# Closing rows with VectorE's copy and a third row begun ahead, and rotation with the sine at the eviction, in a two-layer encoder on one core

## Chip, core and metric

The kernel runs on one core of one Trainium2 chip. The metric is the device time of one execution in microseconds (us): the median of several runs. Engines: PE is TensorE (matmuls and transposes), DVE is VectorE, ACT is ScalarE, POOL is GpSimd, and SP issues the DMA transfers. PE writes its results to PSUM, a small memory of eight banks; DVE and ACT read it from there. The other memory that the engines share is SBUF.

## The reference, cut to what matters

512 tokens of 1024 features pass through two layers, each with three residual additions, and a last norm:

```
for l in range(DEPTH):
    x = x + hybrid_mixer(rms_norm(x, norm_mix[l]), w_in[l], ..., w_out[l])
    x = x + memory_cross_attention(rms_norm(x, norm_mem_q[l]), rms_norm(mem, ...), ...)
    x = x + conv_ffn(rms_norm(x, norm_ffn[l]), w_up[l], conv_w[l], conv_b[l], w_down[l])
return rms_norm(x, norm_final)
```

The mixer has two head groups on one projection. Eight heads do neighbourhood attention over the 8 by 64 token grid (a softmax over 256 neighbours of each block, with a learned bias). Eight query heads and two key heads of 64 features do grouped attention: each head of q and k is normalised over its 64 features and then rotated,

```
out = stack([x1 * c - x2 * sn, x1 * sn + x2 * c])
```

where x1 and x2 are groups of 16 features of the normalised head and c, sn are cosine and sine of a position. Both groups' outputs are put side by side and multiplied by w_out. Everything is float32.

## The kernel before, in words

**Layout.** x lies transposed in SBUF (`xT[c]`, eight tiles of 128 features by 512 tokens). A float32 matrix product is made of three products of rounded parts: each operand is split into hi (rounded) and lo (the rest), and hi times hi, hi times lo and lo times hi are accumulated in one PSUM bank. Weights are read by DMA as `raw`; hi comes from ACT (L265) and lo from POOL (L266), some steps ahead of use. `get_w` takes the next weight of the plan and issues the following transfers and splits.

**Order of the work.** A scheduler decides the order of each engine's instructions from the program's order and priorities; `behind(n)` shifts the priority of what is in it (negative: earlier). Attention is written as a weave: units of work pass through stages (scores, normalise, transpose, values), and between their stages a filler issues pieces of projection matmuls, so that PE has work while the other engines are at softmax. `late(n, f)` calls f n ticks of the filler later. A tick is a few matmuls long.

**PSUM.** Four banks hold matmul results (`mm`), two scores (`sc`), two transposes and small results (`tr`). Accesses of two engines to one bank follow each other in program order, reads too. A bank is free for the next product when its last reader is done.

**Closing rows.** A row is one of eight 128-feature slices of a product that is added to x; 12 matmuls of 512 columns make one. `Norm.close` (L425) is called for 40 rows: the eight of the mixer's output and the eight of memory attention in both layers, and the eight of layer 0's last product. It adds x in PSUM (L428, DVE), makes the next stage's operand hi on ACT (L438) and lo on DVE (L440), copies the sum to `xT` (L430, ACT) and squares it for the norm's statistic (L444, ACT). `close_rows` (L960) runs the last quarter of the mixer's product: rows 0 and 1 are begun when the first two parts of the attention output are there and continued with the third; the fourth part, which goes through `fold` (L481: ACT copy L486, DVE add L488; later ACT L491 and POOL L492), is waited for. When it is there, all eight rows are closed one after the other.

**Neighbourhood values.** `na_values` (L775) multiplies the split values with the split probabilities into a bank whose four parts (two halves of partitions by two terms) must be added: ACT copies one half of partitions out (L789, 64 by 512), DVE adds the other half to it (L790), and DVE adds the two terms (L791).

**Rotation.** Each of four pairs of query heads and the pair of key heads is projected into one bank by `gqa_project`, and then `gqa_rope` (L835) makes three things from it: xs = gain times the bank (ACT, L840), sq = its square (ACT, L841), cc = gain times the bank times the cosine (DVE, L842). One tick later `swap` starts four DMAs that exchange groups of 32 partitions of xs, PE adds the squares of a head with eight small matmuls (operand `pairs`), and DVE makes the variance v (L852, L855). One tick later `rotate` has POOL take the power -1/2 (L862), spread it over rows (L863), multiply the swapped xs by the sine (L864) and add cc (L865). Two ticks later `norm` transposes the rows by a matmul with the identity, and one tick later DVE multiplies and the result is split. `gqa_tables` (L803) scales cosine and sine tables by the mixer norm's factor at the start of a layer (POOL, L805) and makes its square r2 (L807).

## Time and profile before

| what | value |
|---|---|
| runs | 1388.48, 1388.41, 1386.73 us |
| median | 1388.41 us |
| profiled execution | 1388.67 us |
| its span, first to last instruction | 1386.4 us |
| mean granted clock of TensorE | 0.992 |
| ACT copy to xT in a closing row (L430), x38 | 0.590 us |
| ACT square in a closing row (L444), x38 | 0.611 us |
| ACT xs, sq (L840, L841), x10 each | 0.690, 0.590 us |
| DVE cc (L842), x10 | 0.751 us |
| POOL sine product, sum (L864, L865), x10 each | 1.296, 1.287 us |

The profile is of one execution; its times are those of the median run within 0.3 us. A line of the waits names an engine, its operation and line, then what it waited for (engine, tile, line) with total, number and longest in us. A stretch's line has its bounds, its length and then each engine's busy time with the number of instructions, TensorE's granted clock (1.00 is full speed), the DMA engines' share and GB/s. A timeline's line has start, duration, engine, line, operation, output and inputs, shape, and in brackets the engine's idle time before it and what ended it. Names such as `mm`, `tr`, `sc`, `t` (a temporary), `s` (a small tile), `xg` (the operand's halves) and `r` (a rounded tile) are tiles. "ident" is the identity matrix, used to transpose.

### The profile page before, as it was taken

The numbers are of one execution on the slowest core, as the hardware profiler recorded it, in microseconds if no ns is written. First come the engines' busy times: TensorE is split into PE (matmuls) and PEld (weight loads), VectorE is DVE, ScalarE is ACT, GpSimd is POOL, SyncE is SP. The second block draws the span as 40 slices with busy tenths as digits, with TensorE's granted clock in tenths as the row PEclk, the third lists the DMA queues.
The fourth block names the chain that finished last, engine by engine and source line by source line (L and its number), as shares of the span: only waits on it lengthen the run. The fifth ranks groups of instructions, "written<-read, shape, count | busy, mean of one in ns | idle before, by whom it ended". The sixth has DMA issues, their size and how long they took to land.

```text
span 1386.4 us, 19225 instructions
## 1 busy us (share of the span) xinstructions
PE 1355.3 (98%) x7072; PEld 1157.1 (83%) x7072; DVE 838.3 (60%) x1462; ACT 703.8 (51%) x1305; POOL 719.7 (52%) x537
## 2 busy tenths in 40 slices
PE   8999999999999999999999989999999999999997
PEld 7898789787888888888888978898788888888897
DVE  6666666363787187358446557754638833861874
ACT  6766577655443144234557657766654422432441
POOL 2458876635444444444645678756264444444441
PEclk9999999999999999999999999999999999999998
DMA  7753312322333333333356523223133333333331
GB/s 213 202 145 86 86 57 78 92 62 61 106 97 102 91 94 95 101 100 89 109 147 166 139 74 99 62 75 109 54 90 100 91 104 94 90 93 107 95 89 61
DMA packets 218205, 138.83 MB, mean 100 GB/s; under 512 B 6016, under 2 KB 211072, under 8 KB 218112
## 3 DMA queue, kind: packets, MB, share of 16 engines
q1 hardware_dynamic: 217968, 137.60, 34.9%
q8 instruction: 56, 0.92, 0.3%
q14 instruction: 37, 0.30, 0.1%
q10 hardware_dynamic: 144, 0.00, 0.0%
HBM read 125.00 MB, written 2.10 MB: 92 GB/s over the span
## 4 chain that ended last, share of the span: by engine, by line
PE 88%; ACT 4%; DVE 3%; POOL 2%; DMA 2%; issue 1%; SPq 0%; DVEq 0%; ACTq 0%; POOLq 0%
PE mm L77 79%; PE sc L77 5%; PE tr L64 3%; PE tr L77 1%; ACT hi L265 1%; DMA raw<-in_w_in 1%; POOL lo L266 1%; DMA raw<-in_w_down 1%; DVE s L900 1%; POOL r L266 0%; DMA xT<-in_xT 0%; ACT t L902 0%; DVE t L455 0%; DVE xg L473 0%; ACT t L745 0%
## 5 line engine op out<-in xcount | busy, mean ns | idle before, releaser
L266 POOL TENSOR_TENSOR lo<-raw,hi 128x1024 fp32r<-128x1024 f32 (+2 forms) x268 | 499.7, 1876 | 496.0 <-ACT hi L265 476.0
L77 PE MATMUL mm<-xg,hi 128*128 128x512 f32 x1920 | 595.5, 391 | 1.4 <-DVE t L842 1.4
L77 PEld LDWEIGHTS mm<-xg,hi 128*128 128x128 f32 x1920 | 357.4, 188 | 73.3 <-DVE t L842 1.6
L265 ACT CAST hi<-raw 128x512 fp32r<-128x512 f32 (+2 forms) x276 | 224.5, 837 | 349.0 <-PE mm L77 277.5
L77 PE MATMUL mm<-xg,lo 128*128 128x512 f32 x960 | 374.3, 390 | 0.0
L77 PE MATMUL mm<-r,hi 128*128 128x512 f32 (+1 forms) x1144 | 333.9, 376 | 4.4 <-ACT t L444 2.2
L77 PEld LDWEIGHTS mm<-r,hi 128*128 128x128 f32 x1144 | 209.2, 190 | 42.7 <-ACT t L444 3.1
L1202 DVE SCALAR_TENSOR_TENSOR t<-t,par,t 128x7 f32<-128x7 f32 (+1 forms) x352 | 201.9, 641 | 34.0 <-ACT t L1195 34.0
L77 PE MATMUL mm<-r,lo 128*128 128x512 f32 (+1 forms) x572 | 214.3, 375 | 0.0
L77 PEld LDWEIGHTS mm<-xg,lo 128*128 128x128 f32 x960 | 180.7, 188 | 38.1
L77 PEld LDWEIGHTS mm<-r,lo 128*128 128x128 f32 x572 | 108.5, 190 | 19.1
L1187 DVE TENSOR_TENSOR t<-mm,rep 128x512 f32<-128x512 f32 x88 | 60.1, 687 | 78.2 <-PE mm L77 62.3
L479 POOL TENSOR_SCALAR t<-t,s 128x512 f32<-128x512 f32 (+1 forms) x112 | 66.1, 607 | 75.1 <-DVE s L908 37.2
L1204 ACT ACTIVATE t<-t 128x512 f32<-128x512 f32 x44 | 27.9, 633 | 134.5 <-DVE t L1202 134.5
L1208 DVE TENSOR_TENSOR r<-t,r 128x512 fp32r<-128x512 f32 x44 | 90.5, 2056 | 7.3 <-ACT r L1207 4.1
L1231 DVE TENSOR_TENSOR xT<-xT,mm 128x512 f32<-128x512 f32 x32 | 21.9, 685 | 106.8 <-PE mm L77 106.8
L77 PE MATMUL sc<-r,r 128*128 128x256 f32 (+1 forms) x352 | 71.3, 334 | 0.4 <-ACT t L902 0.3
L64 PE MATMUL tr<-ident,t 128*128 128x128 f32 x456 | 63.3, 275 | 8.5 <-DVE r L473 2.8
L1195 ACT ACTIVATE t<-t,par 128x512 f32<-128x512 f32 x88 | 66.8, 806 | 3.2 <-DVE t L1187 3.2
L64 PEld LDWEIGHTS tr<-ident,t 128*128 128x128 f32 x456 | 52.0, 141 | 18.7 <-issue 6.9
L77 PE MATMUL mm<-r,r 128*128 128x256 f32 (+1 forms) x428 | 62.1, 297 | 0.1
L77 PEld LDWEIGHTS mm<-r,r 128*128 128x128 f32 x428 | 56.1, 191 | 2.7 <-POOL r L266 0.3
(155 smaller groups left out, 1598.8 us busy)
## 6 DMA issues: line engine op xcount, KB each, us to landing
raw<-in_w_up SPq DMA_DIRECT2D x88, 512.0 KB, 3.9
raw<-in_w_in SPq DMA_DIRECT2D x33, 512.0 KB, 4.5
raw<-in_w_down SPq DMA_DIRECT2D x32, 448.0 KB, 3.8
raw<-in_w_mem_kv SPq DMA_DIRECT2D x16, 512.0 KB, 3.9
raw<-in_w_down SPq DMA_DIRECT2D x16, 512.0 KB, 4.2
r<-in_bias SPq DMA_DIRECT2D x16, 384.0 KB, 6.2
r<-r SPq DMA_DIRECT2D x22, 256.0 KB, 5.3
raw<-in_w_out SPq DMA_DIRECT2D x8, 512.0 KB, 3.6
```

What stands on the lines that cost most here:

```text
L64: return lambda *a, **k: self.tc.keep_in_program_order(op(*a, **k))
L77: return self.tc.keep_in_program_order(self.engine.matmul(out, lhsT, rhs, **k))
L265: act.copy(hi[:, k], raw[:, k])
L266: (POOL if eng[0] == "P" else DVE).tensor_sub(lo[:, k], raw[:, k], f(hi)[:, k])
L479: eng.tensor_scalar(e, e, sums[:, col : col + 1], 1.0, op0=ALU.mult, op1=ALU.mult)
L900: DVE.tensor_reduce(nmx[:, c], sc[j], axis=AX.X, op=ALU.max, negate=True)
L1187: DVE.tensor_mul(u, us[side], ffn.rep)
L1195: ACT.activation(cc, u, AF.Identity, bias=par[:, l, CB + ch : CB + ch + 1], scale=w[1])
L1202: DVE.scalar_tensor_tensor(cc[:, dst], u[:, src], wi, cc[:, dst], op0=ALU.mult, op1=ALU.add)
L1204: ACT.activation(cs[0], cs[0], AF.Silu)
L1208: DVE.tensor_sub(acts[j][1], cs[0], f(acts[j][0]))
L1231: DVE.tensor_add(xT[m], xT[m], pm)
```

## The change

Four edits:

1. `close` copies the sum to `xT` with DVE, right after the add and ahead of hi and lo; the square reads `xT`.
2. `close_rows` begins a third row (its first three parts) before it closes the first.
3. `na_values` copies only one term's half out with ACT, and DVE adds the other two pieces straight out of PSUM; the tile `tt` goes.
4. In `gqa_rope` the sine is multiplied at the eviction, on DVE, so that the swapped xs needs only the addition; the tables are no longer scaled by the norm's factor. Instead epsilon is scaled (`gqa_eps`): the variance that the norm's own `rsqrt` had made is kept (`mix.var`) and multiplied by the epsilon of q and k. v is then one DVE operation instead of two, and the small matmuls, v, the power and the rows are all in `rotate`, one tick later than before. The sign of the sine table is turned to fit.

The diff, cut to its core:

```diff
@@ Norm
             DVE.tensor_add(pm, pm, xT[c])
+            DVE.tensor_copy(xT[c], pm)
             self.operand(c, src=pm)
-            ACT.copy(xT[c], pm)
-            self.square(c, src=pm)
+            self.square(c)
@@ na_values
-                ACT.copy(th[r], po[64:128])
-                DVE.tensor_add(tt[r], po[0:64], th[r])
-            DVE.tensor_add(o32s[p][...], tt[:, :, 0], tt[:, :, 1])
+                ACT.copy(th[r, :, 0], po[64:128, :, 0])
+                DVE.tensor_add(th[r, :, 1], po[0:64, :, 1], th[r, :, 0])
+                DVE.tensor_add(o32[r], po[0:64, :, 0], th[r, :, 1])
@@ gqa_tables, gqa_eps
-            for i in range(2):
-                POOL.tensor_mul(gtab[0][:, i], gtab[0][:, i], mix.rep)
-            r2.append(small(NB))
-            POOL.tensor_mul(r2[0], mix.rstd, mix.rstd)
+            for i, e in enumerate((EPS, EPS * HD)):
+                DVE.tensor_scalar(geps[:, i], mix.var, e, None, op0=ALU.mult)
@@ gqa_rope
-                ACT.activation(xs, pm, AF.Copy, scale=gain)
+                DVE.scalar_tensor_tensor(xs, pm, gain, gtab[0][:, 1], op0=ALU.mult, op1=ALU.mult)
+                DVE.scalar_tensor_tensor(cc, pm, gain, gtab[0][:, 0], op0=ALU.mult, op1=ALU.mult)
                 ACT.activation(sq, pm, AF.Square)
-                DVE.scalar_tensor_tensor(cc, pm, gain, gtab[0][:, 0], op0=ALU.mult, op1=ALU.mult)
             def swap():
                 xr = tmp()
                 for i in range(4):
                     SP.dma_start(xr[32 * i : 32 * i + 32], xs[32 * (i ^ 1) : 32 * (i ^ 1) + 32])
+                late(1, lambda: rotate(xr))
+            def rotate(xr):
                 pv = ps_t()
                 for b in range(NB):
                     PE.matmul(pv[:, 2 * b : 2 * b + 2], sq[:, b * P : (b + 1) * P], pairs, start=True, stop=True)
-                v = small(2 * NB)
-                DVE.tensor_tensor(v..., pv..., r2[0].unsqueeze(2).to_broadcast([P, NB, 2]), op=ALU.mult)
-                DVE.tensor_scalar(v, v, ..., op0=ALU.mult, op1=ALU.add)
-                late(1, lambda: rotate(xr, v))
-            def rotate(xr, v):
-                r = small(2 * NB)
+                v, r = small(2 * NB), small(2 * NB)
+                DVE.scalar_tensor_tensor(v..., pv..., 1.0 / HD if g == "k" else 1.0, geps[...], op0=ALU.mult, op1=ALU.add)
                 rows = tmp()
                 with behind(-40):
                     POOL.tensor_tensor(r, v, mhalf[:, : 2 * NB], op=ALU.pow)
                     POOL.tensor_copy(rows..., r.unsqueeze(2).to_broadcast([P, 2 * NB, HD]))
-                POOL.tensor_mul(xr, xr, gtab[0][:, 1])
                 POOL.tensor_add(xr, cc, xr)
@@ close_rows
+            def begin(m):
+                if m // 2 == len(w):
+                    w.append(get_w(("outg", 0, m // 2)))
+                rows.append((ps_mm(), w[m // 2], slice(P * (m % 2), P * (m % 2) + P)))
+                gemm_T(*rows[m][:2], ops, range(3), 0, 3, rows[m][2])
+            begin(n)
             for m in range(KC):
-                if m < n:
-                    pm, ws, c = rows[m]
-                    gemm_T(pm, ws, ops, [3], 0, 3, c)
-                else:
-                    ...
-                    gemm_T(pm, w[m // 2], ops, range(4), 0, 3, slice(P * (m % 2), P * (m % 2) + P))
+                if m == len(rows):
+                    begin(m)
+                pm, ws, c = rows[m]
+                gemm_T(pm, ws, ops, [3], 0, 3, c)
                 norm.close(m, pm)
```

The number of matmuls is the same in both kernels.

More of the change, by code (lines that the diff above doesn't have):

```diff
@@ L379, in encoder_kernel @@
     gfin = cpool.tile([P, KC], F32, name="gfin")
+    geps = cpool.tile([P, 2, NB], F32, name="geps")
     def load_parameters():
@@ L403, in rsqrt @@
             POOL.tensor_tensor(r, v, mhalf[:, :n], op=ALU.pow)
-        return r
+        return r, v
     def row_rep(rstd, n, tag, bufs):
@@ L440, in operand, with square @@
                 dve.scalar_tensor_tensor(lo, src, g, f(hi), op0=ALU.mult, op1=ALU.subtract)
-        def square(self, c, act=ACT, eng=None, src=None):
+        def square(self, c, act=ACT, eng=None):
             sq = tmp((self.n,))
-            act.activation(sq, xT[c][:, self.cols] if src is None else src, AF.Square)
+            act.activation(sq, xT[c][:, self.cols], AF.Square)
             eng = eng or (POOL if self.gcol is not None and c < KC - 1 else DVE)
@@ L464, in stat @@
                     PE.matmul(pv[:, b : b + 1], self.last[:, bs], ones, start=False, stop=True)
-            self.rstd = rsqrt(pv[:, 0:nb], nb, 1.0 / D, factor)
+            self.rstd, self.var = rsqrt(pv[:, 0:nb], nb, 1.0 / D, factor)
         def spread(self):
@@ L779, in na_values @@
                 o32s[p] = tmp()
-            th, tt = tmp((2, 2, P)), tmp((2, 2, P))
+            th = tmp((2, 2, P))
+            o32 = o32s[p][:, 256 * bp : 256 * bp + 256].rearrange("p (i q) -> p i q", i=2)
             for j in range(2):
@@ L788, in na_values @@
                 r = slice(64 * j, 64 * j + 64)
-                ACT.copy(th[r], po[64:128])
-                DVE.tensor_add(tt[r], po[0:64], th[r])
-            DVE.tensor_add(o32s[p][:, 256 * bp : 256 * bp + 256].rearrange("p (i q) -> p i q", i=2), tt[:, :, 0], tt[:, :, 1])
+                ACT.copy(th[r, :, 0], po[64:128, :, 0])
+                DVE.tensor_add(th[r, :, 1], po[0:64, :, 1], th[r, :, 0])
+                DVE.tensor_add(o32[r], po[0:64, :, 0], th[r, :, 1])
             if bp == 1:
@@ L797, in na_values, with gqa_eps @@
                     vblk[p // 2] = None
-        gq, gk, gvt, gtab, r2 = [None] * 4, [], [], [], []
-        def gqa_tables():
-            for i in range(2):
-                POOL.tensor_mul(gtab[0][:, i], gtab[0][:, i], mix.rep)
-            r2.append(small(NB))
-            POOL.tensor_mul(r2[0], mix.rstd, mix.rstd)
+        gq, gk, gvt, gtab = [None] * 4, [], [], []
+        def gqa_eps():
+            for i, e in enumerate((EPS, EPS * HD)):
+                DVE.tensor_scalar(geps[:, i], mix.var, e, None, op0=ALU.mult)
         def gqa_project(g):
@@ L850, in swap @@
                     PE.matmul(pv[:, 2 * b : 2 * b + 2], sq[:, b * P : (b + 1) * P], pairs, start=True, stop=True)
-                v = small(2 * NB)
-                DVE.tensor_tensor(v.rearrange("p (b j) -> p b j", j=2), pv[:, 0 : 2 * NB].rearrange("p (b j) -> p b j", j=2),
-                                  r2[0].unsqueeze(2).to_broadcast([P, NB, 2]), op=ALU.mult)
-                DVE.tensor_scalar(v, v, *((1.0 / HD, EPS) if g == "k" else (1.0, EPS * HD)), op0=ALU.mult, op1=ALU.add)
-                late(1, lambda: rotate(xr, v))
-            def rotate(xr, v):
-                r = small(2 * NB)
+                v, r = small(2 * NB), small(2 * NB)
+                DVE.scalar_tensor_tensor(
+                    v.rearrange("p (b j) -> p b j", j=2), pv[:, 0 : 2 * NB].rearrange("p (b j) -> p b j", j=2),
+                    1.0 / HD if g == "k" else 1.0, geps[:, int(g != "k")].unsqueeze(2).to_broadcast([P, NB, 2]),
+                    op0=ALU.mult, op1=ALU.add)
                 rows = tmp()
@@ L978, in close_rows @@
             norm = norm()
-            for m in range(KC):
-                if m < n:
-                    pm, ws, c = rows[m]
-                    gemm_T(pm, ws, ops, [3], 0, 3, c)
-                else:
-                    if m // 2 == len(w):
-                        w.append(get_w(("outg", 0, m // 2)))
-                    pm = ps_mm()
-                    gemm_T(pm, w[m // 2], ops, range(4), 0, 3, slice(P * (m % 2), P * (m % 2) + P))
+            def begin(m):
[4 more added lines that the diff above has]
+            begin(n)
+            for m in range(KC):
+                if m == len(rows):
+                    begin(m)
+                pm, ws, c = rows[m]
+                gemm_T(pm, ws, ops, [3], 0, 3, c)
                 norm.close(m, pm)
@@ L1034, in na_quanta @@
                 SP.dma_start(gtab[0], t["rope"])
-                gqa_tables()
+                gqa_eps()
             return [NA_FILL] * 3
@@ L1312, in _rope_tables @@
     c, s = np.cos(ang).reshape(S, 2 * nf).T, np.sin(ang).reshape(S, 2 * nf).T
-    tab = np.stack([np.concatenate([c, c, c, c]), np.concatenate([-s, s, -s, s])], axis=1)
+    tab = np.stack([np.concatenate([c, c, c, c]), np.concatenate([s, -s, s, -s])], axis=1)
     return np.ascontiguousarray(tab.astype(np.float32))
```

## The prediction

> **What bounds the kernel now.** I read the page first (busy shares, the chain that ended last), then the waits of PE, then the stretches around each wait, then the timelines of PE, ACT, POOL and DVE there. The profiled execution took 1388.67 us, 0.26 over the median of 1388.41; its span is 1386.4, so 2.3 us lie around it. All sums below are made against 1388.67.

> ```profile
> PE 1355.3 (98%) x7072; PEld 1157.1 (83%) x7072; DVE 838.3 (60%) x1462; ACT 703.8 (51%) x1305; POOL 719.7 (52%) x537
> ...
> PE 88%; ACT 4%; DVE 3%; POOL 2%; DMA 2%; issue 1%; SPq 0%; DVEq 0%; ACTq 0%; POOLq 0%
> ```

> PE is the bound. The change issues the same matmuls, so only PE's stalls can move, and the other engines count only where one of them is late for PE. The waits of PE (engine, line, waited for: total, times, longest):

> ```profile
> PE tr L64 <- DVE r L473: 2.8, 2, 1.9
> PE tr L77 <- ACT t L841: 2.6, 2, 1.3
> PE mm L77 <- ACT t L444: 2.2, 2, 1.1
> PE tr L64 <- DVE xg L473: 2.0, 2, 1.6
> PE mm L77 <- POOL r L492: 1.9, 1, 1.9
> ...
> PE mm L77 <- DVE t L842: 1.4, 1, 1.4
> ...
> PE tr L64 <- POOL t L479: 1.3, 2, 0.8
> PE mm L77 <- POOL t L863: 1.2, 1, 1.2
> ```

> Nearly all of them lie in four places that the diff touches: the rotary part (L841, L842, L863, and transposes queued near it), the closing rows (L492, L444). A stall has a second price, seen in PE's stretches cut at 3.41 us (busy times of PE, PEld, DVE, ACT, POOL; then the granted clock):

> ```profile
> 145.52:148.93 3.41, 2.18 (x9) 2.18 (x10) 2.26 (x6) 1.97 (x5) 3.41 (x4) 0.50 0.73 190
> 247.92:251.33 3.41, 1.32 (x7) 0.80 (x6) 0.48 (x1) 2.13 (x5) 3.41 (x4) 1.00 0.00 0
> 251.33:254.75 3.42, 3.42 (x9) 2.69 (x9) 2.05 (x3) 0.99 (x2) 2.14 (x2) 0.50 0.54 161
> 817.95:821.36 3.41, 1.50 (x10) 1.20 (x9) 2.53 (x5) 2.18 (x6) 1.44 (x2) 1.00 0.32 72
> 821.36:824.77 3.41, 3.41 (x10) 2.61 (x9) 2.05 (x3) 1.00 (x2) 2.55 (x2) 0.50 0.02 5
> 841.84:845.25 3.41, 1.77 (x11) 1.30 (x10) 3.33 (x6) 3.38 (x9) 3.41 (x7) 1.00 0.09 22
> 845.25:848.66 3.41, 3.41 (x18) 2.87 (x19) 2.90 (x6) 2.57 (x7) 3.41 (x4) 1.00 0.00 0
> ```

> The stretches that follow 1.32 and 1.50 us of busy PE ran at clock 0.50; the one that follows 1.77 ran at 1.00. In the half-clock stretches PE lost a further 1.9 us (251.3), 1.4 (821.4) and 1.95 (148.5 to 152.3), by the excess of its start-to-start times over the usual 0.227 us of a 512-column matmul. So a stall near 1.9 us costs about 3.5 in all, one of 1.6 only itself. [...]

> **The closing rows, one row.** Before: DVE add 0.70 (L428), ACT hi 0.69 (L438), DVE lo 0.75 (L440), ACT copy 0.59 (L430), ACT square 0.61 (L444), which frees the bank: 3.34 us. After: the copy is on DVE and stands ahead of hi. No row shows a DVE copy out of PSUM; its bounds are 0.42 (L488, an add on half the columns) and 0.75 (L440), and I take 0.69, by the row it is nearest to, L428's add of the same shape. Square now reads SBUF and holds no bank. [...] The bank is freed at 0.70 + 0.69 + 0.69 + 0.75 = 2.83 us, 0.5 earlier, while lo, which the next stage reads, is 0.7 later. DVE's load per row goes from 1.45 to 2.14 us, under PE's 2.72 (12 matmuls), so DVE does not become the bound; without that margin each of 40 rows would add the excess.

> At 322.4 and 1000.65 PE waited 1.28 us each for L444 to free a bank. The first bank now comes 0.3 earlier: **-0.6** for both (nothing to -1.0).

> **The third row, layer 0.** The timeline there:

> ```profile
> 247.80 2.52 POOL L266 TENSOR_TENSOR lo<-raw,hi 128x512 fp32r<-128x512 f32 x2 [5.36 <-ACT hi L265]
> ...
> 250.28 0.71 POOL L492 TENSOR_TENSOR r<-t,r 128x256 fp32r<-128x256 f32 x1
> ...
> 251.05 0.58 PE L77 MATMUL mm<-r,hi 128*128 128x512 f32 x1 [1.95 <-POOL r L492]
> ```

> The last part of the third k waits on POOL's fold, which stands behind two weight folds. The loss was 0.30 + 2.22 + 1.9 at half clock = 4.4. After, nine matmuls of the third row (9 x 0.227 = 2.04 us) run from about 248.46 to 250.50, and 0.5 is left, with no half clock: -3.9. But the order of ACT's instructions changes: the split of the first memory-query weight (L265) now stands ahead of the first row's hi, since hi waits for one more DVE step.

> ```profile
> 252.83 0.69 ACT L438 ACTIVATE xg<-mm,par 128x512 fp32r<-128x512 f32 x1 [2.75 <-DVE mm L428]
> 254.45 1.05 ACT L265 CAST hi<-raw 128x1024 fp32r<-128x1024 f32 x1 [0.94 <-DMA raw<-in_w_mem_q]
> ```

> That split waits for a DMA that landed at 254.45 (issued at 250.34, when POOL freed the raw tile, which the change does not move). So hi of row 0 runs from 255.5 to 256.2, lo to 256.95, and the fifth row, which needs the first row's bank at about 255.55, waits 1.4. Net **-2.5** (-3.9 if the split does not hold hi back, -0.8 if this stall takes the clock too).

> **The same in layer 1.** There is no stall to win. In that layer too the split (937.00 to 938.05, waiting for its DMA) now stands ahead of hi; hi ends at 938.75, lo at 939.5, and the fifth row wants the bank at 937.76: **+1.75** (0 to +3.45, with 1.7 for a half-clock stretch; 1.75 lies between the 1.64 that did not set it off and the 1.91 that did).

> **The neighbourhood values.** ACT's copy goes from 0.58 (L789) to 0.37 (L486, the same shape), 32 times; DVE's 0.68 + 0.43/2 becomes 2 x 0.42 (L488). ACT gains 6.7 us beside PE, DVE breaks even, PE waits for neither at this line: 0. If their cover were gone this would be worth 0.2 a unit.

> **The rotary part.** POOL loses ten multiplications of 1.30 (L864) and four of 1.30 (L805), 18 us beside PE. DVE takes xs at 0.75 (nearest row L842; L840 on ACT took 0.69), ACT keeps sq, now behind both DVE reads. Bank and pairs operand come within 0.1 of before (0.75 + 0.75 + 0.59 against 0.69 + 0.59 + 0.75). The pairs' eight small matmuls, the one DVE step on them (0.17 to 0.22 by L852, L855, where two stood), POOL's power (1.65) and rows (0.62) are issued one tick later, so PE's wait for sq (142, 830) goes, but POOL's power now queues behind two more weight folds of 1.25 (L266). SP's swap transfers stay where they were.

> Layer 0: the stalls at 100.9 (0.40), 110.5 (0.13) and 133 (1.03), and 0.9 at the pairs, go by the order: some 2.4 up to the last projection, which ends at T0 = 141.1. From there, before: the last norm (ident matmuls) at T0 + 11.6. After, counted from an end 2.4 earlier: POOL's L266 pair to +3.2, power to +4.85, rows to +5.5; PE is there at +2.75, so it stalls about 2.7, probably with a half-clock stretch; the last norm comes at +12.3 to 13, which is T0 + 9.9 to 10.6. Gain 1.0 to 1.7. The wait for L479 at 162 (1.18) is filled by six more matmuls: gain 1.0. Together **-2.4** (-4 to +0).

> Layer 1, an estimate with the same rows: the waits at 817.9 (2.07, and 1.4 of clock) and 830.1 (1.49) go: -4.96. New: the third q head's norm waits 2.2 for POOL's rows (which come 5.5 after the end of the last projection, PE at 3.2), half the time with a stretch of 1.7 (+0.85), and transposes behind DVE's later step, the two small score products that stood ahead of them covering 0.96 of it: +0.96. The 1.8 at 843 stays. Net **-1.0** (-5 to +4).

> Sum: -2.5 + 1.75 - 0.6 - 2.4 - 1.0 = -4.75, so 1388.67 - 4.75 = 1383.9. FFN (340 to 690, 1020 to 1340) loses nothing before and nothing after.

> **Rivals.**
> 1. *The weight split in front of hi costs a clock stretch in both layers.* -2.5 + 1.7, +1.75 + 1.7, the rest as above: -1.35, 1387.3: no change to measure. For it: 1.75 is near the edge. Against: 1.4 is not.
> 2. *The late tick of the pairs: POOL's rows hold PE at the norms of the last two q heads.* Decides from where rows come over 1.9 after PE. In layer 1, where neither norm waited before, 2.2 and 2.4 with 1.65 of clock each are +7.9 against -4.96: +2.9; layer 0 comes out at 0, and the fifth row in layer 1 takes its stretch: -2.5 + 3.45 - 0.6 + 0 + 2.9 = +3.25, so 1391.9, slower. For it: POOL is busy for all 3.41 us of the stretch at 841.84. Against: POOL has 1.30 less to do for each head.
> 3. *The split does not hold hi back* (its DMA lands earlier, or hi is off the path): -3.9 + 0 - 0.6 - 2.4 - 1 = -7.9, and with layer 1 at -3, -9.9: about 1379.
> 4. *The change does not do what it says:* the third row could be begun too late to cover the fold. The order of PE's instructions puts its nine matmuls ahead of the last parts, and the bank that they need came free at 247.36, so I give this nothing; it would be the forecast without -3.9 + 1.4 = 2.5, or 1386.4.

> **How the numbers follow.** Forecast 0.48, rival 1 0.20, rival 2 0.22, rival 3 0.10. Time 1383.9. The range 1379 to 1393 takes in rivals 1 and 2 and the edge of 3; the open bounds of the rotary part alone are some 9 us wide. About 0.2% (2.8 us) is what a measurement of this kernel can tell from no change. Faster: forecast, rival 3, less the forecast's upper edge: 0.55; within: 0.21; slower: 0.24.

> **What would show it.** In the changed kernel: no wait for L492's fold over 0.6 and clock 1.00 after 251; ACT's weight split ahead of the first L438 at both closings and a fifth row waiting 1.4 and 1.75 for lo; waits for L444's square gone from PE's list and replaced by lo's line at 0.9 to 1.0; no PE wait for sq; instead norms waiting for POOL's rows. Wrong would be: half-clock stretches at 255 or 938, DVE as the releaser of every closing row, or norms of layer 1 that wait over 2 us twice.

## The result and the profile after

| | before | changed |
|---|---|---|
| median of 8 runs | 1388.28 us | 1383.66 us |
| range | 1385.84 to 1388.8 | 1381.91 to 1386.0 |
| ratio to before, 95% interval | | 0.9972 [0.9963, 0.9981] |
| profiled execution, its span | 1388.67, 1386.4 us | 1382.43, 1380.3 us |

The change takes off 0.28%, 4.6 us by the medians. In the page's busy times and the chain of the changed kernel

```profile
PE 1352.6 (98%) x7072; PEld 1155.5 (84%) x7072; DVE 862.9 (63%) x1522; ACT 673.4 (49%) x1255; POOL 701.9 (51%) x521
...
PE 91%; DVE 3%; ACT 2%; DMA 2%; POOL 1%; issue 1%; SPq 0%; DVEq 0%; ACTq 0%; POOLq 0%
```

PE still bounds it, with the same 7072 instructions. DVE has 25 us more, ACT 30 and POOL 18 less. The time goes by where one of them is late for PE, so PE's waits come next:

```profile
PE mm L77 <- POOL t L865: 5.2, 2, 2.7
PE mm L77 <- DVE xg L441: 2.6, 4, 1.2
...
PE sc L77 <- ACT t L903: 1.6, 3, 0.9
...
PE tr L77 <- DVE t L543: 1.3, 1, 1.3
...
PE mm L77 <- POOL r L493: 0.3, 1, 0.3
```

(The line numbers are one or two higher than before: L865 is the copy of POOL's rows, L863 before; L441 is lo of a closing row, L493 the fold.) Gone are the waits for sq (2.6 us), for the bank that cc held (1.4), for the closing square (2.2) and most of the fold's (1.9). New are two long waits for POOL's rows (before, one of 1.2), four for lo in closing rows, and waits of the grouped attention behind them.

A measure that goes through all texts below is PE's loss: for each matmul the time from its start to the next one's start, less the median of that time for its shape in the kernel before, added up by stage (negative: faster than the median). It holds waits and half-clock time together. A single wait that the text gives is counted in the same way; PE's idle time in a timeline's brackets is 0.1 to 0.3 us less. "Rotary" are the stages of both attention groups (45 to 240 us and 690 to 925), "closing" the mixer's closing rows (240 to 262, 925 to 945), "memory" what follows them up to the feed-forward part.

| profile of | rotary, layer 0 | closing 0 | memory 0 | rotary, layer 1 | closing 1 | memory 1 | all else |
|---|---|---|---|---|---|---|---|
| before | 12.0 | 4.2 | 2.8 | 12.1 | 0.0 | 2.8 | 9.3 |
| changed | 10.9 | 1.7 | 2.1 | 11.3 | 1.5 | 2.1 | 8.0 |

Of the 5.7 us of loss between the two profiles (their spans differ by 6.1), 4.4 lie in stages that the diff touches. The 1.3 under "all else" lie at the start and the end, which no edit touches; the loss up to 45 us varies from 5.6 to 7.1 among the profiles of this document.

The closing rows of layer 0 and layer 1 (timelines of ACT, DVE and PE of the changed kernel, two places):

```profile
252.62 1.05 ACT L265 CAST hi<-raw 128x1024 fp32r<-128x1024 f32 x1 [4.07 <-DMA raw<-in_w_mem_q]
253.57 0.68 ACT L439 ACTIVATE xg<-mm,par 128x512 fp32r<-128x512 f32 x1
...
255.09 0.74 PE L77 MATMUL mm<-r,hi 128*128 128x512 f32 x2 [0.69 <-DVE xg L441]
```

```profile
930.80 1.05 ACT L265 CAST hi<-raw 128x1024 fp32r<-128x1024 f32 x1 [4.02 <-DMA raw<-in_w_mem_q]
931.76 0.68 ACT L439 ACTIVATE xg<-mm,par 128x512 fp32r<-128x512 f32 x1
...
932.47 0.75 DVE L441 SCALAR_TENSOR_TENSOR xg<-mm,par,xg 128x512 fp32r<-128x512 f32 x1 [0.69 <-ACT xg L439]
...
933.28 0.73 PE L77 MATMUL mm<-r,hi 128*128 128x512 f32 x2 [1.21 <-DVE xg L441]
```

ACT stands still for 4 us before a weight's DMA with the first row's hi behind it; lo comes after hi, and PE's fifth row waits for lo. The clock of PE after the fold in layer 0, and after the first wait for POOL's rows (stretches; the third value from the end is the clock):

```profile
250.90:254.30 3.40, 3.40 (x16) 2.55 (x14) 3.21 (x7) 1.68 (x3) 1.67 (x2) 1.00 0.56 168
...
145.25:148.66 3.41, 3.41 (x11) 2.73 (x11) 1.81 (x4) 1.16 (x2) 3.41 (x3) 0.55 1.09 361
```

No half-clock stretch follows the fold any more; one now follows the rows (0.50 from 145.57 to 148.99).

### The profile page after: what moved, and what is told of

It reads as the page before. It is cut to its first block, busy times and chain, and to the rows that moved or that the text cites. A ratio compares the mean times of both kernels' runs of the same rounds, so it can differ in the third digit from the quotient of the medians.

```text
span 1380.3 us, 19215 instructions
## 1 busy us (share of the span) xinstructions
PE 1352.6 (98%) x7072; PEld 1155.5 (84%) x7072; DVE 862.9 (63%) x1522; ACT 673.4 (49%) x1255; POOL 701.9 (51%) x521
## 4 chain that ended last, share of the span: by engine, by line
PE 91%; DVE 3%; ACT 2%; DMA 2%; POOL 1%; issue 1%; SPq 0%; DVEq 0%; ACTq 0%; POOLq 0%
PE mm L77 82%; PE sc L77 5%; PE tr L64 3%; PE tr L77 1%; DMA raw<-in_w_in 1%; ACT hi L265 1%; POOL lo L266 1%; DMA raw<-in_w_mem_q 1%; DVE xg L474 0%; DVE s L901 0%; DVE t L456 0%; DVE mm L429 0%; DVE t L542 0%; SPq L64 0%; DVE xT L430 0%
## 5 line engine op out<-in xcount | busy, mean ns | idle before, releaser
L266 POOL TENSOR_TENSOR lo<-raw,hi 128x1024 fp32r<-128x1024 f32 (+2 forms) x268 | 499.0, 1874 | 516.0 <-ACT hi L265 513.6
L77 PE MATMUL mm<-xg,hi 128*128 128x512 f32 x1920 | 594.3, 391 | 0.0
L77 PEld LDWEIGHTS mm<-xg,hi 128*128 128x128 f32 x1920 | 356.8, 188 | 71.9 <-ACT t L845 0.2
L265 ACT CAST hi<-raw 128x512 fp32r<-128x512 f32 (+2 forms) x276 | 224.2, 836 | 369.4 <-PE mm L77 301.9
L77 PE MATMUL mm<-xg,lo 128*128 128x512 f32 x960 | 373.8, 389 | 0.0
L77 PE MATMUL mm<-r,hi 128*128 128x512 f32 (+1 forms) x1144 | 333.1, 375 | 3.0 <-DVE xg L441 2.6
L77 PEld LDWEIGHTS mm<-r,hi 128*128 128x128 f32 x1144 | 208.3, 190 | 42.1 <-DVE xg L441 4.3
L77 PE MATMUL mm<-r,lo 128*128 128x512 f32 (+1 forms) x572 | 213.7, 374 | 0.0
L77 PEld LDWEIGHTS mm<-xg,lo 128*128 128x128 f32 x960 | 180.2, 188 | 38.0
L77 PEld LDWEIGHTS mm<-r,lo 128*128 128x128 f32 x572 | 108.3, 189 | 19.1
L77 PE MATMUL sc<-r,r 128*128 128x256 f32 (+1 forms) x352 | 72.5, 338 | 1.6 <-ACT t L903 1.6
L64 PE MATMUL tr<-ident,t 128*128 128x128 f32 x456 | 61.9, 274 | 4.8 <-DVE xg L474 1.7
L64 PEld LDWEIGHTS tr<-ident,t 128*128 128x128 f32 x456 | 52.3, 140 | 13.3 <-issue 3.5
L77 PE MATMUL mm<-r,r 128*128 128x256 f32 (+1 forms) x428 | 61.8, 297 | 0.0
L77 PEld LDWEIGHTS mm<-r,r 128*128 128x128 f32 x428 | 56.1, 191 | 2.4
```

The lines of the kernel that those rows point to most:

```text
L64: return lambda *a, **k: self.tc.keep_in_program_order(op(*a, **k))
L77: return self.tc.keep_in_program_order(self.engine.matmul(out, lhsT, rhs, **k))
L265: act.copy(hi[:, k], raw[:, k])
L266: (POOL if eng[0] == "P" else DVE).tensor_sub(lo[:, k], raw[:, k], f(hi)[:, k])
```

## Experiments

Theory A: each edit acts in its own stage, as the prediction's terms have it. The rivals are named with each run. Ratios are to the kernel before, run beside them.

### The four edits, one at a time

Each is one part of the diff above on the kernel before: the close alone

```diff
+            DVE.tensor_copy(xT[c], pm)
             self.operand(c, src=pm)
-            ACT.copy(xT[c], pm)
-            self.square(c, src=pm)
+            self.square(c)
```

the third row alone

```diff
+            begin(n)
             for m in range(KC):
+                if m == len(rows):
+                    begin(m)
```

the values alone

```diff
-                ACT.copy(th[r], po[64:128])
+                ACT.copy(th[r, :, 0], po[64:128, :, 0])
+                DVE.tensor_add(th[r, :, 1], po[0:64, :, 1], th[r, :, 0])
+                DVE.tensor_add(o32[r], po[0:64, :, 0], th[r, :, 1])
```

and the rotation alone, with the scaled epsilon and the turned table:

```diff
-                late(1, lambda: rotate(xr, v))
+                late(1, lambda: rotate(xr))
-                POOL.tensor_mul(xr, xr, gtab[0][:, 1])
```

> The kernel before with the closing rows' copy on DVE alone (two rows begun ahead, old values, old rotation). Theory A, each edit acts in its own stage: the first bank of memory attention's closing rows comes earlier, -0.7 us in each layer; in layer 1's mixer closing the weight split stands ahead of the first hi and the fifth row waits about 1.7 us for lo; in layer 0's the fifth row is wanted some 2.5 us later than lo is done, so nothing changes there and the wait for the fold (2.2 us and a half-clock stretch) stays. Sum about +0.3 us, no change to measure. Rival B, the earlier release of the banks is what won in all closings: layer 0's closing loses 1.5 to 2.5 us less, sum -2.5 to -4.

> The kernel before with the third row begun ahead alone (copy and square stay on ACT, reading PSUM). Theory A: the fold's wait in layer 0 falls from 2.2 to about 0.5 us and the half-clock stretch goes, -3.9; but the first row now ends only two rows' last parts and one row ahead of the fifth row, and ACT's copy and square of row 0 stand behind the weight split that waits for its DMA (to 255.5) and two further hi, so the fifth row waits about 2.5 us: -1.4 in layer 0; in layer 1 the same order costs about +1.4. Sum about 0. Rival B, the split holds up only hi behind the DVE copy, so that the third row alone is pure gain: -3.9 in layer 0 and 0 in layer 1.

> The kernel before with the new neighbourhood values alone. Theory A: PE waits at no place for these lines, ACT's 6.7 us less lies beside PE: within 0.5 us of before, and PE's stalls at 100.9, 133, 162 and 817.9 stay as they are. Rival B: the stalls of the neighbourhood stage that went in the changed kernel (0.40, 0.13 and 1.03 us in layer 0) went because ACT and DVE were relieved here: -1 to -1.6 us, and those stalls are gone.

> The kernel before with the new rotation alone. Theory A: the order of PE's work alone takes the stalls at 100.9, 110.5, 133, 142 (layer 0), 817.9 and 830.1 (layer 1), and the later tick brings one wait of about 2.8 us with a half-clock stretch for POOL's rows in each layer, as in the changed kernel: stretch 45 to 185 us loses about 1.5 us less, 690 to 852 about 1 us less, sum -1.5 to -3. Rival B: the gain needs the relieved ACT of the values too, and the later tick alone costs more than it brings: +1 to +3, with waits for POOL's rows over 2 us at more than one norm of a layer.

| edit alone | median, us | ratio, interval | rotary 0 | closing 0 | memory 0 | rotary 1 | closing 1 | memory 1 |
|---|---|---|---|---|---|---|---|---|
| close | 1385.31 | 0.9985 [0.9976, 0.9994] | 11.9 | 4.2 | 2.0 | 11.4 | 0.0 | 2.1 |
| third row | 1388.25 | 1.0010 [1.0001, 1.0019] | 12.1 | 2.6 | 2.8 | 10.4 | 2.0 | 2.8 |
| values | 1389.59 | 1.0015 [1.0006, 1.0024] | 12.4 | 4.3 | 2.8 | 12.4 | 0.0 | 2.8 |
| rotation | 1386.77 | 0.9999 [0.9990, 1.0008] | 13.4 | 2.6 | 2.8 | 12.4 | 0.0 | 2.7 |

Multiplied, the four ratios give 1.0009, where all four together gave 0.9972: 0.37% comes from how they act on one another. Two pairs come into question. By the ratios, all of it lies in the second: values and rotation give 1.0014 multiplied and 0.9976 together (below), while close and third row give 0.9995 multiplied, and the change over that pair is 0.9972 / 0.9976 = 0.9996. Each ratio is known to about 0.1%.

The values alone were a miss: the median is 1.9 us longer, where I had expected at most 0.5 either way. Its profile is the fastest of its executions and shows 0.3 us more loss in all, so where the rest lies is not seen. A single column can move without an edit: the third row touches nothing in the rotary stages, yet its profile loses 10.4 us there in layer 1 where the kernel before loses 12.1. Both have the wait of 2.1 us near 820 (1.9 of it idle). In the kernel before, a half-clock stretch follows it (0.50 from 821.36 to 824.77, 1.51 us of loss); the mean clock of the third row's profile is 0.994 against 0.992, which would fit one that did not come. Differences of up to 1.7 us in one column may be such a stretch, by my estimate from these numbers.

**Close and third row.** The close alone gains (0.8 and 0.7 us in the memory stages) and costs nothing in the mixer's closings. In layer 0 of that kernel ACT has the same order as in the changed one,

```profile
254.42 1.05 ACT L265 CAST hi<-raw 128x1024 fp32r<-128x1024 f32 x1 [4.26 <-DMA raw<-in_w_mem_q]
255.38 0.68 ACT L438 ACTIVATE xg<-mm,par 128x512 fp32r<-128x512 f32 x1
```

and yet no fifth row waits: with two rows begun ahead it is wanted nine matmuls (2.04 us) later after the first row's end. In this profile closing 0 loses 4.2 us, as in the kernel before, where a half-clock stretch (0.50 from 251.33 to 254.75) has its part in that and delays the fifth row too; but the changed kernel with two rows (below) has the same order, the split at 251.84 and hi at 252.80, a clock of 1.00 from 248.80 to 255.60, and no wait either. In layer 1 with two rows hi even runs ahead of the split,

```profile
932.43 0.69 ACT L438 ACTIVATE xg<-mm,par 128x512 fp32r<-128x512 f32 x1 [1.36 <-DVE xT L429]
...
935.60 1.05 ACT L265 CAST hi<-raw 128x1024 fp32r<-128x1024 f32 x1 [0.86 <-DMA raw<-in_w_mem_q]
```

so the +1.7 that I expected there did not come. The third row alone makes PE wait in both layers, 1.84 and 1.88 us, though hi of row 0 is there before the split; there it is the copy and the square that come behind it, and the square frees the bank (ACT, then PE, layer 1):

```profile
930.63 1.37 ACT L438 ACTIVATE xg<-mm,par 128x512 fp32r<-128x512 f32 x2 [1.98 <-DVE mm L428]
933.00 1.05 ACT L265 CAST hi<-raw 128x1024 fp32r<-128x1024 f32 x1 [1.00 <-DMA raw<-in_w_mem_q]
933.95 0.68 ACT L438 ACTIVATE xg<-mm,par 128x512 fp32r<-128x512 f32 x1
934.53 0.58 ACT L430 COPY xT<-mm 128x512 f32<-128x512 f32 x1
935.00 0.61 ACT L444 ACTIVATE t<-mm 128x512 f32<-128x512 f32 x1
...
935.66 0.72 PE L77 MATMUL mm<-r,hi 128*128 128x512 f32 x2 [1.72 <-ACT t L444]
```

So the price in layer 1 belongs to the third row: it takes its 2.04 us out of the time between the first row's end and the fifth row's start, and then anything of row 0 that stands behind the split on ACT is late.

**Values and rotation.** Each alone lost more in the rotary stages of layer 0 than the kernel before (by 0.4 and 1.4 us). The rotation alone has a wait of 1.95 us (in the last line below) that neither the kernel before nor the changed one has. PE, DVE and again PE there:

```profile
120.50 1.05 PE L77 MATMUL mm<-ident,t 128*128 128x128 f32 x8
...
121.66 1.38 DVE L791 TENSOR_TENSOR t<-mm,t 64x512 f32<-64x512 f32 x2 [2.14 <-PE mm L77]
...
124.40 0.15 DVE L857 SCALAR_TENSOR_TENSOR s<-tr,geps 128x8 f32<-128x8 f32 x1
...
124.61 0.66 PE L64 MATMUL tr<-ident,t 128*128 128x128 f32 x4 [1.78 <-DVE s L857]
```

DVE's addition of the values stood idle for 2.14 us although ACT's copies had ended at 118.7: it waited for PE's eight transposes of a head's rows, which end just before it starts. My reading is that its output tile `tt` was the buffer that they still had to read: twelve temporaries go round, and the later tick keeps sq and the rows in theirs for longer. Behind the addition stood v, and for v's bank PE's transposes waited. The changed values have no `tt`.

### Is it the temporary tile?

```diff
-            th, tt = tmp((2, 2, P)), tmp((2, 2, P))
+            th = tmp((2, 2, P))
-                DVE.tensor_add(tt[r], po[0:64], th[r])
+                DVE.tensor_add(th[r], po[0:64], th[r])
```

(on the rotation alone, and the last addition reads th; beside it values and rotation together)

> The kernel before with the new rotation, and in the old neighbourhood values the sum tt written in place of th: the same copies and additions with the same sizes, but one temporary tile less. The rotation alone had a new wait of 1.95 us at 122.6 and one of 1.93 at 149.6. Theory A, the temporaries: the later tick keeps sq and rows one tick longer, the values' tt then waits for a tile that PE's norm reads, and DVE's queue stands behind it; with tt gone the wait at 122.6 goes, as in the changed kernel, and the sum is about 2 us faster than the rotation alone. Rival B, the values' shorter copy on ACT is what takes it away: here the wait stays.

> The kernel before with the new values and the new rotation, the closing rows as before. Theory A, the two edits gain only together: stretches 45 to 185 us lose about 1.7 us less than before and 690 to 852 about 0.5 less, and the closings as before (4.2 us in layer 0, 0 in layer 1): -2 to -2.5 us, though each alone gave nothing. Rival B, there is no such tie and the gain of the changed kernel comes from the closing rows: 0 within 0.8.

With one tile less the wait fell from 1.95 to 0.78 us, so the tile was the larger part of this wait. But the kernel was not faster: 1386.27 us, 0.9997 [0.9988, 1.0006], and its loss in the rotary stages (13.2 and 12.9) is no smaller than the rotation's. Values and rotation together: 1383.88 us, 0.9976 [0.9968, 0.9985], with 10.9 and 11.3, the same as in the changed kernel. Theory A holds for the pair, not in the form that the tile alone explains it. The two runs differ only in the form of the values, so the 2.4 us between their medians come from the shorter copies and additions; how these divide between ACT and DVE, and by which waits they act, stays open.

### The copy behind hi and lo; the pairs back in the earlier tick

On the changed kernel, the copy last:

```diff
-            DVE.tensor_copy(xT[c], pm)
             self.operand(c, src=pm)
+            DVE.tensor_copy(xT[c], pm)
             self.square(c)
```

and the pairs early:

```diff
             def swap():
...
-                late(1, lambda: rotate(xr))
+                pv = ps_t()
+                for b in range(NB):
+                    PE.matmul(pv[:, 2 * b : 2 * b + 2], sq[:, b * P : (b + 1) * P], pairs, start=True, stop=True)
+                v = small(2 * NB)
...
+                late(1, lambda: rotate(xr, v))
```

> The changed kernel with DVE's copy to xT put behind hi and lo of its row instead of ahead of them; nothing else differs, and ACT then has the first row's hi ahead of the weight split that waits for its DMA. Theory A, the fifth row of each closing waits (0.85 us in layer 0, 1.37 in layer 1) since the copy put that split in front of hi, while the third row took 2.04 us from the time between the first row's end and the fifth row's start: both waits fall to 0.4 us or less, and the kernel is 1.2 to 2 us faster than the changed one. Rival B, DVE's queue (three adds and a copy ahead of the first lo) is what holds the bank: the waits stay within 0.3 us of what they are.

> The changed kernel with the pairs' small matmuls and v back in the tick of the swap (power and rows stay where they are). Theory A, the later tick causes PE's two waits for POOL's rows (2.77 and 2.82 us, each with a half-clock stretch of some 1.7) and takes away the waits for sq: the first two go, the waits for sq (1.4 to 1.5 us in each layer) come back, and with them some transposes' waits of 1 to 2 us: sum 0 to -3 us against the changed kernel. Rival B, POOL's rows are late for another reason (weight folds ahead of them): both waits of about 2.8 us stay.

**Copy last:** 1379.7 us, 0.9944 [0.9931, 0.9956], about 4 us below the changed kernel, twice what I had expected. Both closings lose nothing any more at the fifth row (0.7 and 0.0 in all), and the memory stages fall from 2.1 to 1.5 each. ACT in layer 1:

```profile
927.14 1.37 ACT L439 ACTIVATE xg<-mm,par 128x512 fp32r<-128x512 f32 x2 [1.98 <-DVE mm L429]
929.32 1.05 ACT L265 CAST hi<-raw 128x1024 fp32r<-128x1024 f32 x1 [0.81 <-DMA raw<-in_w_mem_q]
```

Two rows' hi now run while the DMA is under way. Rival B, DVE's queue, falls: DVE does the same work in another order. The gain in the memory stages I had not expected; hi no longer waits for the copy there either.

**Pairs early:** 1377.54 us, 0.9930 [0.9917, 0.9944], more than I had given it. The wait for POOL's rows in layer 1 is gone, and in layer 0 the first one; one of 2.34 us came at the last norm, and the waits for sq (1.34 and 1.44) are back. In the closing of layer 1, which the edit does not touch, the fifth row's wait for lo grew from 1.37 to 2.19 us, and a half-clock stretch follows it (clock 0.74 from 931.0 to 934.4). So the profiled execution, 1382.05 us at a mean clock of 0.992, is no faster than the changed kernel's profile. The other four had 0.996 or 0.997 and took 1376.9 to 1379.5 us. Fewer half-clock stretches would fit that, but these four have no profile, so where they gained is not shown. Why the rows are late in the changed kernel, by POOL's timeline there:

```profile
138.69 2.54 POOL L266 TENSOR_TENSOR lo<-raw,hi 128x512 fp32r<-128x512 f32 x2 [2.93 <-ACT hi L265]
141.18 1.65 POOL L864 TENSOR_TENSOR s<-s,mhalf 128x8 f32<-128x8 f32 x1
...
142.90 0.61 POOL L865 COPY t<-s 128x512 f32<-128x512 f32 x1
```

A pair of weight folds goes ahead of the power; before 138.69 POOL had been idle for 2.93 us. With the pairs one tick earlier the power runs in that idle time (from 137.09 to 138.74 in the kernel with both mends, below).

### Together, and what the third row is worth

Two rows, on the changed kernel and on the one with both mends (copy last and pairs early):

```diff
-            begin(n)
             for m in range(KC):
```

and on the one with both mends, sq first:

```diff
             with behind(-20):
+                ACT.activation(sq, pm, AF.Square)
                 DVE.scalar_tensor_tensor(xs, ...)
                 DVE.scalar_tensor_tensor(cc, ...)
-                ACT.activation(sq, pm, AF.Square)
```

> The changed kernel with only two rows begun ahead, as before; all else as changed. Theory A, the third row gives in layer 0 about what it takes in layer 1: with two rows the fold's wait of 2.2 us is back in layer 0 (and a half-clock stretch after it in some executions), the fifth row's waits (0.85 and 1.37) are gone: 0 to +1.5 us against the changed kernel. Rival B, the third row is what the change lives on: +2.5 us or more.

> The changed kernel with both mends: the copy behind hi and lo, and the pairs and v in the swap's tick. Theory A, they act in different stages and add up: the fifth rows wait 0.4 us or less, no wait of 2.8 us for POOL's rows, -3.9 and -5 of the two alone: about 1375 us, ratio to before 0.990 to 0.9915. Rival B, the faster closings bring a later wait (a weight split or its DMA), and less than half of the smaller gain is seen: 1376.5 or more.

> As the kernel with both mends, and in the rotation ACT's square stands ahead of DVE's two reads of the bank instead of behind them. Theory A, PE's waits for sq at the pairs (1.34 us in layer 0, 1.44 in layer 1) are the price of sq's place behind two reads of 0.75: both go, a wait for POOL's rows grows by at most 0.6 (xs and cc come that much later): -1 to -2.5 us against the kernel with both mends. Rival B, ACT's queue and not the bank's order holds sq (a split or a copy stands ahead of it): the waits stay over 1 us.

> As the kernel with both mends, with two rows begun ahead. Theory A, once hi stands ahead of the weight split the third row costs nothing in layer 1, so taking it away loses its whole gain in layer 0: +1.7 us (the wait for the fold from 0.5 back to 2.2), and up to +3.4 where a half-clock stretch follows. Rival B, the third row gives nothing here either: within 0.7 us.

| kernel | median, us | ratio, interval | rotary 0 | closing 0 | rotary 1 | closing 1 |
|---|---|---|---|---|---|---|
| changed, copy last | 1379.7 | 0.9944 [0.9931, 0.9956] | 10.9 | 0.7 | 11.4 | 0.0 |
| changed, pairs early | 1377.54 | 0.9930 [0.9917, 0.9944] | 10.7 | 1.5 | 9.0 | 4.0 |
| changed, two rows | 1381.46 | 0.9958 [0.9946, 0.9971] | 10.9 | 2.7 | 11.1 | 0.0 |
| both mends | 1374.8 | 0.9909 [0.9896, 0.9923] | 9.1 | 0.7 | 9.1 | 0.0 |
| both mends, sq first | 1383.11 | 0.9973 [0.9963, 0.9983] | 14.7 | 0.7 | 12.6 | 0.0 |
| both mends, two rows | 1376.99 | 0.9920 [0.9907, 0.9934] | 10.7 | 4.3 | 9.0 | 0.0 |

Both mends together: 1374.8 us, 12.7 below the kernel before, the fastest version here and what I had expected (about 1375). By the medians they nearly add up; in the profiles the copy last also takes away the long fifth-row wait that the early pairs had. What is left of PE's waits there:

```profile
PE tr L77 <- ACT t L845: 2.5, 2, 1.3
PE mm L77 <- POOL t L866: 2.2, 1, 2.2
PE tr L64 <- DVE xg L474: 2.1, 2, 1.7
```

The third row in the changed kernel gained nothing: without it the median is 2.2 us lower, where I had expected 0 to 1.5 higher (the intervals overlap, so it may be less, but no gain is seen). With both mends it is worth about 2.2 us by the medians (1374.8 against 1376.99). There the intervals overlap too. Closing 0 differs by 3.6 us in the profiles, 1.7 of it the fold's wait and most of the rest a half-clock stretch (clock 0.62 from 248.45 to 251.86); one execution without the third row, at a mean clock of 0.997, took 1374.75 us.

Sq first was a miss. The waits for sq became shorter (0.84 and 0.88), but xs comes later, its swap's DMA too, and POOL's order turned:

```profile
147.58 1.28 POOL L867 TENSOR_TENSOR t<-t,t 128x512 f32<-128x512 f32 x1 [0.76 <-DMA t<-t]
148.84 1.36 POOL L480 TENSOR_SCALAR t<-t,s 128x512 f32<-128x512 f32 x2
...
150.72 1.26 POOL L501 TENSOR_TENSOR r<-t,r 128x512 fp32r<-128x512 f32 x1
```

POOL idles for the DMA, and the lo part of the neighbourhood output (L501) ends at 152.0 instead of 146.5; PE waited 3.8 us for it. That the scheduler puts other work ahead is visible; which of these steps made it do so was not tried.

## Why the prediction came out, point by point

1. **PE's waits alone decide.** Right: the busy times of DVE, ACT and POOL moved by 18 to 30 us, and the span (6.1 us less) followed PE's loss (5.7 less).
2. **DVE's copy, 0.69.** It took 0.680 (L430, 38 times). The gain at the memory closings was mis-sized: -0.6 forecast for both, and PE's wait fell from 1.28 to 0.51 in each, -1.5 together, outside the range of nothing to -1.0; the release came 0.77 earlier, not 0.3. The prediction's own sum for one row gives 0.5 and does not say why 0.3 was taken.
3. **Third row in layer 0, -2.5.** Measured 4.2 to 1.7, -2.5. Its parts: the fold's wait 0.50 (0.5 forecast), no half clock (1.00 from 250.90 to 254.30), and the fifth row's wait 0.85 (1.4 forecast; the DMA landed at about 252.6, some 0.5 us earlier against PE's row than I had worked out). In the measure of the tables the half-clock stretches of before from 251.33 and 821.36 cost 1.56 and 1.51 us, and the one from 145.52 to 152.35, twice as long, 2.75; the prediction has 1.9, 1.4 and 1.95 (the last from 148.5 on).
4. **Layer 1, +1.75.** Measured +1.5, with the split ahead of hi as forecast. The step that failed is the cause: the prediction put the whole price on the copy that moves hi behind the split. The copy alone cost nothing, the third row alone 2.0, and with the copy behind hi the third row costs nothing either. So the price needs both: less time up to the bank's next use, and something of the first row behind the split on ACT. The prediction never counted that a row begun ahead shortens the way to the bank's next use.
5. **Values, 0.** Alone it was not a gain; it came out slightly slower (1.0015, the interval is above 1), where 0 was forecast. That nothing else leans on them was wrong: the rotation's gain is only there with them, 10.9 against 13.4 us of loss in layer 0. The prediction looked for waits at their lines and not for who needs their buffers and DVE's time.
6. **Rotary part, -2.4 and -1.0.** Measured -1.1 and -0.9. The waits that were to go went (133, 142, 817.9's larger part, 830), and the rows' new waits came where they were put: 2.7 forecast and 2.77 measured in layer 0, 2.2 and 2.82 in layer 1, each with a half-clock stretch (0.50 from 145.57 to 148.99, and in layer 1 for twice 3.41 us, from 824.83 to 831.65). The step that failed in layer 0 is the term of 1.0 for the wait at 162: it did go, but scores and small products that follow wait instead (1.11 up to 166.35, 1.42 up to 172.04). From 160 to 240 us PE lost 1.3 more than before, where 1.0 less was forecast; up to 160 it lost 2.3 less, where 1.0 to 1.7 was forecast.
7. **The sum, 1383.9.** Measured 1383.66. By stages the forecast -4.75 stands against -4.4 in the profiles, but the agreement is in part luck: +1.3 in the rotary part of layer 0 and -0.8 in the memory stages largely cancel. The rival of the late tick was right about its mechanism and wrong about its size: one wait for POOL's rows came in each layer, where it had two in layer 1.

## What to carry to other kernels

Work begun ahead on an engine that is the bound takes its time out of some other buffer's grace (here 2.04 us of the time to the next use of the first row's bank): after finding the wait that it fills, count the time between the last use of each bank and its next use again. An edit that is worth nothing alone may free what another one needs, such as a temporary tile or time in an engine's queue (here the values alone 1.0015 and the rotation alone 0.9999, both together 0.9976); edits with terms that "lie beside PE" are worth a run in pairs. Ahead of an instruction that waits for a DMA, put what others are waiting for: here one line's place (copy ahead of or behind hi) was worth nearly as much as the whole change (4.0 us by the medians, the change 4.6).

## What the runs showed of the hardware

```profile
248.80:252.20 3.40, 3.37 (x15) 2.80 (x16) 2.54 (x4) 0.36 (x1) 2.47 (x2) 1.00 0.54 159
```

```profile
248.45:251.86 3.41, 3.38 (x10) 2.68 (x11) 2.19 (x4) 1.05 (x2) 2.45 (x2) 0.62 0.52 154
```

So the further 1.6 us came in 4 of 6, where the prediction's 1.9 was taken as certain. Between 50 and 1355 us half the clock begins in the kernel before at 145.52, 251.33 and 821.36, which lie 31 and 167 times 3.413 us apart, and in the changed kernel at 145.57 and 824.83, 199 times 3.413 us apart: in each of the two profiles on one grid. Cut on this grid, the stretch ahead of each beginning has 2.15, 1.32 and 1.50 us of busy PE before, and 2.01 and 1.07 in the changed kernel:

```profile
142.16:145.57 3.41, 2.01 (x17) 2.01 (x18) 2.14 (x6) 1.26 (x4) 3.06 (x5) 1.00 0.82 240
145.57:148.98 3.41, 3.41 (x9) 2.63 (x9) 1.52 (x3) 1.13 (x2) 3.41 (x3) 0.50 1.07 361
...
821.41:824.82 3.41, 1.07 (x5) 0.54 (x3) 0.72 (x2) 1.44 (x4) 3.35 (x4) 1.00 0.47 123
824.83:828.24 3.41, 3.11 (x15) 3.11 (x15) 0.70 (x1) 0.21 (x1) 2.83 (x4) 0.50 1.05 316
```

The two profiles have 755 such stretches at full clock in that time. The three with 1.50 us or less of busy PE were followed by half the clock, and none with more than 2.15. Of the five between, two were (2.15 before, 2.01 in the changed kernel), and three were not (1.77 before; 1.80 and, from 169.47, 2.15 in the changed kernel), so busy time alone does not decide it. The 1.91 and 1.64 us that the prediction sets beside its 1.75 are the 3.41 of a stretch less 1.50 and 1.77.

In the rotation alone, where closing 0 lost 2.6 us, the stretches on either side of 250.18 share the idle time, and both are at full clock (PE's busy time is the first after the length):

```profile
246.77:250.18 3.41, 2.36 (x17) 1.84 (x15) 1.23 (x3) 2.88 (x6) 2.21 (x2) 1.00 0.02 5
250.18:253.59 3.41, 2.37 (x10) 1.99 (x11) 1.53 (x3) 0.75 (x2) 3.41 (x4) 1.00 0.53 143
```

That a wait so divided draws no half clock was not shown: in the changed kernel the wait of 2.77 us for POOL's rows in layer 0 is divided too (2.22 us of busy PE from 138.75, 2.01 from 142.16), and half the clock followed, with 1.5 us of loss. The waits of 1.8 us that remain near 840 drew it in neither profile: the stretches that hold most of them have 1.77 us of busy PE before and 1.80 in the changed kernel, and the next ones ran at 1.00.
